# Chunk steps one turn sooner, attention's tile pool split, four kinds of stores on other queues: a change to a hybrid Hyena / mLSTM encoder layer

## The chip, the core and the metric

The kernel runs on one core of a Trainium2 chip. The metric is device time in microseconds (us). The kernel before takes 3098.87 us, the median of 3 runs (3091.53 to 3103.35).

A core has five engines that run side by side, each with its own instruction queue that is worked off in order: TensorE (PE in the profile; PEld are its weight loads), VectorE (DVE), ScalarE (ACT), GpSimd (POOL) and SyncE (SP). In this kernel before the change, SP and ACT are the queues from which transfers are issued; an issue is an instruction like any other, so an engine that waits before an issue holds up everything behind it. SPq and ACTq in the profile are the issuing sides of these two.

## What is computed

One encoder layer, sequence length 2048, model width 1024, all in float32:

```
u = rms_norm(x) ;  P = u @ w_in                      # 1024 x 3600
hy = conv3(P[:, :1536]) ;  spec = filter spectrum(sin-FFN)
y_hy = group_norm( x2 * (h2 * z1 + d2 z1) ),  z1 = x1 * (h1 * v + d1 v)    # long convolutions by FFT
q, k = silu(conv3(P[:, 1536:2560])) ;  v, o, gates = the rest of P
y_ml = group_norm( sigmoid(o) * (mlstm(q,k,v,gates) + mlstm backwards) )  # 4 heads of 128, in chunks
h = x + concat(y_hy, y_ml) @ w_out
h = h + cross_attention(rms_norm(h), rms_norm(mem))  # 4 heads of 256, 256 memory rows
h = h + relu(rms_norm(h) @ ff_w1)^2 @ ff_w2          # 1024 -> 4096 -> 1024
out = rms_norm(h)
```

## The kernel before

Nearly every large product is made from three matmuls: each operand is split into a rounded high half (by ScalarE) and the remainder (by VectorE), and high x high, high x low and low x high are added in PSUM (`mm3`, lines 355 to 361; `split`, line 367).

The kernel is written with Tile: the program allocates tiles from named pools, and a scheduler orders the instructions of every engine from a simulated timeline and puts in the waits. A tile with `bufs=n` has n places that are used in turn. Pools lie on a stack: a pool opened after others were closed takes over their addresses, and its tiles wait until what lay there has been released. A change of a pool or of one step therefore lets the scheduler order all instructions anew.

The program (lines 2078 to 2115) weaves generators. Each `yield` is a turn; `weave(a, b, wa, wb)` takes turns of a and b so that their yielded amounts advance in the ratio wa : wb. The stages that matter here:

- **Input projection** (`sweep`, `natural`): 14 column groups of w_in against the 2048 rows, 1024 rows at a time. `natural` stores the values `vd`, the sigmoid output gate `od` and the gates; its stores of `vd` and `od` go out from ScalarE's queue (line 888). Beside it run the filters, then the Hyena convolution (`hyena`), whose last step stores the normed rows `yh` from SP's queue (line 1058), eight pairs of stores. Every pair touches rows all over the sequence, so the whole of `yh` is complete only with the last.
- **Memory projection** (`memproj`, lines 689 to 742): 8 steps, one for each head's keys and each head's values. A step takes a raw 1024 x 256 weight (`project`, 32 matmuls at line 704), copies the result (`kt`, line 706), multiplies it by a second weight (`keys`, line 721, or `values`, line 733), copies each PSUM bank into a staging tile `o` (tag `st`, 3 places, line 711) and stores it from ScalarE's queue: `gd` for the keys (line 723, 16 stores), `vw` for the values (line 735, 16 stores). The weights (`wm`) come in through SP's queue (line 417), into four places.
- **mLSTM chunks** (`mlstm`, from line 1217): 16 chunks of 128 rows in a chain. One chunk goes through SP loads (lines 1248, 1249, 1168, 1174), matmuls (1274, 1312, 1314, 1190), GpSimd (1280, 1281, 1333), ScalarE (1283, 1317, 1326, 1184) and VectorE (1265, 1284, 1320, 1328, 1196); every second chunk is followed by the norm of two chunks and their stores `ym` (line 1348). The first call of the generator sets the constants up, loads two chunks and makes the first scores; each later call does one chunk.
- **The join**: `take(n, 2)` runs two turns of the memory projection, then `beside_each(n, take(m, 5))` alternates one turn of it with one of the first five of the mLSTM. So four chunks are done when the first block of the next stage wants their 512 rows.
- **Attention** (`attention`, from line 1418), in four blocks of 512 rows. A block turns the rows of `yh` and `ym` by transposes (`mixed`, `rows`, `turn`, lines 1452 to 1477), multiplies by w_out (8 products), then scores, softmax, weighing with `vw`, 8 more products, residual, and `store`, which scales one 128 x 512 piece (`hg`, 2 places, line 1602) and stores it from ScalarE's queue (line 1603, 32 stores in all). Weights come as pairs of 8 KB tiles a partition, `wh` and `wl`, two places each; each 256 KB piece is loaded by SP into a staging tile (`wn`, four places, shared with the rows; the first pair through the tag `e`) and split. The first block starts with the half of its products that needs only `yh` (line 1512).
- The mLSTM's other chunks are woven into the attention by `weave(g, m, 440, 112, True)`.
- **Feed-forward** (`ffn`): 2 x 7 products of a Strassen-like scheme up and down; it fills the last 1200 us.

The pools on the left side of the stack before: `i_sb` holds everything of the input projection and the memory projection (the parameters, `P`, `cv`, `xn`, `wh`, `wl`, `wn`, `st`, ...). Above it lie the small gate columns and `h_sb`, the Hyena's pool. When all these are closed, `t` takes the addresses over, with acc, the second pair of row tiles (`act1`), both weight pairs, and, as they are first used, the first pair of row tiles (`act0`) and `wn`. `t_a` (staging `e`, `hg`, sums) is on top.

Of the kernel before, what the change touches and what calls it, by code (L numbers as in the profile page):

```python
# [20 lines left out]
D = 1024  # L21
# [112 lines left out]
class Prog:  # L134
# [247 lines left out]
    def weights(self, pool, w, n, kc=4, bufs=2, nbufs=2, pin=False):  # L382
# [4 lines left out]
        if n > 512:  # L387
            for k0 in range(kt):
                for c0 in range(0, n, 512):
                    cs = slice(c0, c0 + 512)  # L390
                    nat = pool.tile([128, 512], F32, tag="wn", name="wn", bufs=nbufs)
# [3 lines left out]
        for k0 in range(0, kt, kc):  # L395
            nat = pool.tile([128, kc, n], F32, tag="wn", name="wn", bufs=nbufs)
# [31 lines left out]
    def inproj_open(self, es):  # L428
# [7 lines left out]
        self.d_gt = self.dram("gt", (L, 16))  # L436
        sb = self.isb = es.enter_context(tc.tile_pool(name="i_sb", bufs=1))
# [27 lines left out]
    def square_sum(self, x, dst):  # L465
        junk = self.isb.tile([128, 512], F32, tag="st", name="junk", bufs=3)
        return self.tc.keep_in_program_order(self.nc.scalar.activation(junk, x, AF.Square, accum_out=dst))
# [56 lines left out]
    def x_chunks(self, hf):  # L524
# [3 lines left out]
        def room(n):  # L528
            if not 1 < n < deep:
                return None  # L530
            t = self.isb.tile([128, 1088], F32, tag=("P", "cv")[n % 2], name="xt", bufs=2)
# [16 lines left out]
    def x_first(self):  # L548
# [18 lines left out]
        for j in range(4):  # L567
            t = sb.tile([128, 1088], F32, tag=("P", "cv")[j // 2], name="xt", bufs=2)
# [13 lines left out]
        def squares(xs, c):  # L582
            for k in range(8):
                sq = sb.tile([128, 512], F32, tag="st", name="sq", bufs=3) if k else ssum[c]
# [33 lines left out]
        def second():  # L618
            for k in range(0, 8, 2):
                nat = sb.tile([128, 2, 256], F32, tag="wn", name="wn", bufs=4)  # L620
# [40 lines left out]
    def prep_mem(self):  # L661
# [11 lines left out]
        def halves():  # L673
            xs = [load(h) for h in range(2)]
            by_half = self.dram("rows", (2, 128, 128)).rearrange("i (d s n h) t -> s (i d) n (h t)", d=2, s=2, n=8)
            t = sb.tile([128, 1088], F32, tag="cv", name="rp", bufs=2)[:, 0:D]
# [12 lines left out]
    def memproj(self):  # L689
# [19 lines left out]
        def staged(p):  # L709
            o = sb.tile([128, 2, 256], F32, tag="st", name="o", bufs=3)  # L710
            nc.scalar.copy(o, p)
            return o

        def keys(h, t):
            q = next(self.mst)
            for i2 in range(4):
# [6 lines left out]
                nc.scalar.dma_start(out=gd[h // 2, :, 2 * i2:2 * i2 + 2, cs], in_=staged(p))  # L723
# [20 lines left out]
    def sweep(self, cols, hf, first, after=None):  # L744
# [3 lines left out]
        for run in [cols[:2]] + [[c2] for c2 in cols[2:]] if self.made == 0 else [[c2] for c2 in cols]:  # L748
# [7 lines left out]
            for c, c2 in [(c, c2) for c in range(2) for c2 in run]:  # L756
                wh, wl = ws[c2]
                for m in range(2):
# [11 lines left out]
                    def leave(c=c, m=m, c2=c2, p=p, cc=cc, Ps=Ps, run=run):  # L770
# [19 lines left out]
                        cv = sb.tile([128, 1088], F32, tag="cv", name="cv", bufs=2)  # L790
# [20 lines left out]
    def sweep_out(self, ct, cv, t0, n):  # L811
# [3 lines left out]
        if ct < 12:  # L815
            w = min(n // 8, 128)
            dst = self.d_hy[ct // 4, t0:t0 + 8 * w, cc].rearrange("(q j) c -> q j c", j=8)
            for j4 in range(2):
# [3 lines left out]
                st = sb.tile([128, 4, 128], F32, tag="st", name="st", bufs=3)  # L822
                self.copy(st[0:w], pt[0:w])
                nc.sync.dma_start(out=dst[:, 4 * j4:4 * j4 + 4], in_=st[0:w])
            if n > 8 * w:
                pt = self.mm()
                nc.tensor.transpose(pt[0:16, 0:128], v[:, 8 * w:n], self.ident)
                st = sb.tile([128, 4, 128], F32, tag="st", name="st", bufs=3)
# [7 lines left out]
        for b in range(0, n, 512):  # L836
            pt = self.mm().rearrange("p (k t) -> p k t", k=4)
            st = sb.tile([128, 4, 128], F32, tag="st", name="st", bufs=3)
# [9 lines left out]
            if rest:  # L848
# [3 lines left out]
                st = sb.tile([128, 4, 128], F32, tag="st", name="st", bufs=3)  # L852
# [3 lines left out]
    def natural(self, hf, tiles, after=None, at=4):  # L856
# [3 lines left out]
        for c2 in tiles:  # L860
# [3 lines left out]
            for t in range(8):  # L864
# [18 lines left out]
                so = sb.tile([128, 512], F32, tag="st", name="st", bufs=3)[:, 0:256]  # L883
# [4 lines left out]
                nc.scalar.dma_start(out=(self.d_vd if c2 < 2 else self.d_od)[r0:r0 + 128, 256 * (c2 % 2):256 * (c2 % 2) + 256],  # L888
# [1282 lines left out]
```

## Time and profile before

| | us |
|---|---|
| median of 3 runs | 3098.87 |
| lowest, highest | 3091.53, 3103.35 |
| the profiled execution | 3097.53 |
| its span, first to last instruction | 3095.8 |
| TensorE matmuls busy | 3023.0 |
| VectorE, ScalarE, GpSimd busy | 1952.6, 1500.4, 1130.9 |

The profile page gives one execution. "Busy" is the union of an engine's instructions. The windows view cuts the span into stretches and gives for each engine its busy time (with the number of instructions), the TensorE clock that was granted (1.00 is full speed), the mean busy share of the 16 DMA engines and the GB/s they moved; a share can come out slightly over 1. The view of waits says which engine stood idle before a line and what ended the idle time, with the total, the number of times and the longest, all in us. The chain of waits walks back from the last instruction through what released each step. In a timeline a row has the start, the time taken, the engine, the line, the operation, its tiles, and in brackets the idle time before it and its releaser. The releaser is the semaphore event that came last, so it can be a transfer that has nothing to do with the data.

### The profile page before, as it was taken

What the parts mean: (1) busy time and instruction counts of PE and PEld (TensorE: products, weight loads), DVE (VectorE), ACT (ScalarE), POOL (GpSimd) and SP (SyncE); (2) the same over time, 40 slices, a digit from 0 to 9 for tenths busy, and PEclk for the clock granted to TensorE, in tenths of its full rate; (3) what the DMA queues carried; (4) which work ended last, traced back from release to release, by engine and by line L of the source; (5) the groups of instructions that cost most, each with busy time, mean ns of one, the idle gap of its engine ahead of it and who ended that gap; (6) DMA issues with size and microseconds to landing.
All of it is one profiled execution on the core that took longest, in us unless ns stands there. A gap on an engine that the chain in (4) does not pass through costs nothing.

```text
span 3095.8 us, 42982 instructions
## 1 busy us (share of the span) xinstructions
PE 3023.0 (98%) x14287; PEld 2375.2 (77%) x14287; DVE 1952.6 (63%) x3442; ACT 1500.4 (48%) x2930; POOL 1130.9 (37%) x798
## 2 busy tenths in 40 slices
PE   9999999999999998999999999999999999999998
PEld 7655767776676766888887888888888888888876
DVE  8855465446656456877664666557555686566695
ACT  6443465534656225565544455556555543333335
POOL 0122011200222343333132237766466374244653
PEclk9999999999999999999999999999999999999999
DMA  6554767575867997464476556657544565353434
GB/s 225 187 191 164 243 214 237 178 234 193 260 199 241 301 309 231 151 204 160 149 246 222 183 188 224 210 180 240 196 153 151 183 212 171 109 166 117 159 102 164
DMA packets 444102, 607.07 MB, mean 196 GB/s; under 512 B 38494, under 2 KB 248542, under 8 KB 442856
## 3 DMA queue, kind: packets, MB, share of 16 engines
q1 hardware_dynamic: 405988, 546.54, 55.1%
q10 hardware_dynamic: 37892, 57.79, 5.5%
q8 instruction: 113, 1.85, 0.2%
q14 instruction: 109, 0.89, 0.1%
HBM read 401.79 MB, written 202.41 MB: 195 GB/s over the span
## 4 chain that ended last, share of the span: by engine, by line
PE 82%; DMA 7%; DVE 5%; ACT 2%; issue 2%; POOL 1%; SPq 0%; ACTq 0%; DVEq 0%; POOLq 0%
PE mm L357 17%; PE mm L361 17%; PE mm L360 17%; PE hy L357 6%; PE hy L361 6%; PE hy L360 6%; PE hy L178 3%; PE mm L948 2%; PE hy L979 1%; PE hy L1021 1%; DMA a<-hy 1%; DMA xt<-in_x_t_dram 1%; PE hy L1312 1%; PE mm L733 1%; PE hy L1314 1%
## 5 line engine op out<-in xcount | busy, mean ns | idle before, releaser
L1669 ACT CAST ah<-w 128x512 fp32r<-128x512 f32 x284 | 177.1, 624 | 302.0 <-PE hy L360 155.3
L1670 DVE TENSOR_TENSOR bl<-wr,bh 128x512 fp32r<-128x512 f32 x213 | 238.2, 1123 | 124.7 <-ACT bh L1669 124.7
L368 DVE TENSOR_TENSOR wl<-wn,wh 128x512 fp32r<-128x512 f32 (+1 forms) x296 | 215.4, 773 | 101.1 <-ACT wh L368 100.8
L1026 POOL TENSOR_TENSOR b<-b,a 128x512 f32<-128x512 f32 x64 | 86.8, 1359 | 510.5 <-ACT b L1024 240.8
L357 PE MATMUL mm<-xh,wh 128*128 128x512 f32 x640 | 265.5, 416 | 2.5 <-ACT st L206 1.3
L360 PE MATMUL mm<-xl,wh 128*128 128x512 f32 x640 | 252.9, 395 | 1.8 <-DVE xl L368 1.8
L361 PE MATMUL mm<-xh,wl 128*128 128x512 f32 x640 | 253.6, 397 | 0.0
L1670 DVE TENSOR_TENSOR al<-w,ah 128x512 fp32r<-128x512 f32 x236 | 216.4, 917 | 57.1 <-ACT ah L1669 56.9
L1669 ACT CAST bh<-wr 128x512 fp32r<-128x512 f32 x232 | 143.8, 622 | 223.6 <-PE mm L361 173.8
L361 PE MATMUL mm<-bh,al 128*128 128x512 f32 x576 | 223.7, 391 | 3.8 <-DVE al L1670 3.8
L357 PE MATMUL mm<-bh,ah 128*128 128x512 f32 x576 | 225.8, 392 | 0.8 <-DVE acc L1832 0.7
L360 PE MATMUL mm<-bl,ah 128*128 128x512 f32 x576 | 224.9, 390 | 0.0
L368 ACT CAST wh<-wn 128x512 fp32r<-128x512 f32 (+1 forms) x296 | 165.0, 619 | 104.6 <-PE mm L361 52.6
L360 PE MATMUL mm<-act,wh 128*128 128x512 f32 x512 | 201.8, 394 | 0.0
L361 PE MATMUL mm<-act,wl 128*128 128x512 f32 x512 | 199.3, 391 | 0.4 <-DVE wl L368 0.4
L357 PE MATMUL mm<-act,wh 128*128 128x512 f32 x512 | 198.7, 394 | 1.0 <-ACT wh L368 0.9
L357 PE MATMUL hy<-bh,ah 128*128 128x512 f32 x448 | 175.2, 391 | 0.0
L360 PE MATMUL hy<-bl,ah 128*128 128x512 f32 x448 | 174.6, 390 | 0.0
L361 PE MATMUL hy<-bh,al 128*128 128x512 f32 x448 | 174.4, 390 | 0.0
L357 PEld LDWEIGHTS mm<-xh,wh 128*128 128x128 f32 x640 | 120.1, 188 | 56.0 <-issue 19.2
L357 PE MATMUL mm<-wh,xh 128*128 128x256 f32 (+1 forms) x512 | 155.6, 304 | 3.5 <-ACT xh L368 2.0
L361 PEld LDWEIGHTS mm<-xh,wl 128*128 128x128 f32 x640 | 120.1, 188 | 46.2 <-issue 21.8
(380 smaller groups left out, 8219.6 us busy)
## 6 DMA issues: line engine op xcount, KB each, us to landing
wr<-hc SPq DMA_DIRECT2D x224, 256.0 KB
w<-in_ff_w_dram SPq DMA_DIRECT2D x172, 256.0 KB
hc<-wn SPq DMA_DIRECT2D x128, 256.0 KB
wn<-in_w_in_dram SPq DMA_DIRECT2D x100, 256.0 KB
hc<-q SPq DMA_DIRECT2D x96, 256.0 KB
fs<-a SPq DMA_DIRECT2D x32, 512.0 KB
a<-fs SPq DMA_DIRECT2D x64, 256.0 KB
a<-zs SPq DMA_DIRECT2D x64, 256.0 KB
```

Of the source, the lines that this page charges most:

```text
L178: b = self.nc.tensor.matmul(*products[-1], start=True, stop=True)
L357: first = mm(ps, lh, rh, start=start, stop=False)
L360: mm(ps, lh, rl, start=False, stop=False)
L361: self.last = mm(ps, ll, rh, start=False, stop=stop)
L368: both = (self.nc.scalar.copy(hi, src), self.nc.vector.tensor_tensor(lo, src, hi.bitcast(F32), ALU.subtract))
L733: mul(p, t[:, m, ms], o_[:, m, ds], start=m == 0, stop=m == 1)
L948: nc.tensor.matmul(pp, dm[:, m], t[:, m], start=True, stop=True)
L979: nc.tensor.matmul(pg, em[:, m], y, start=True, stop=True)
L1021: nc.tensor.matmul(pp, dm[:, m], t[:, m], start=True, stop=True)
L1026: nc.gpsimd.tensor_tensor(xt, xt, hi[:, m], ALU.mult)
L1669: self.nc.scalar.copy(hi, src)
L1670: eng.tensor_tensor(lo, src, hi.bitcast(F32), ALU.subtract)
```

## The change

Six edits. The diff is cut to its core; every other use of the tags `st`, `wn` and `cv` in the input projection goes to the new pools in the same way.

1. The input projection's pool is split: `i_w` (tags `cv`, `wn`) at the bottom, then `i_st` (tag `st`), then `i_sb` with the rest.
2. Attention's pool `t` becomes four: `t_w` (the first weight pair) at the bottom, `t_acc`, `t` (the second pair of row tiles and the second weight pair), and `t_n` (the first pair of row tiles, `wn`) on top. Weight pairs alternate between `t_w` and `t`.
3. The stores of `gd`, of `hg` and half of those of `od` (column group 2) move from ScalarE's queue to SP's; those of `yh` move from SP's to GpSimd's. Half of the staged keys use the tag `wn` instead of `st`, so that there are seven places.
4. `take(n, 1)` in place of `take(n, 2)`: each of the first five mLSTM turns comes one turn of the memory projection sooner.
5. `weave(g, m, 440, 140, True)` in place of 112: more mLSTM turns to a product of the attention.
6. In the first block, the first transpose of the `ym` rows is kept in program order.

```diff
+        sw = self.isw = es.enter_context(tc.tile_pool(name="i_w", bufs=1))
+        for tag, n, bufs in (("cv", 1088, 2), ("wn", 544, 4)):
+            for _ in range(bufs):
+                sw.tile([128, n], F32, tag=tag, name=tag, bufs=bufs)
+        self.ist = es.enter_context(tc.tile_pool(name="i_st", bufs=1))
         sb = self.isb = es.enter_context(tc.tile_pool(name="i_sb", bufs=1))
...
-        def staged(p):
-            o = sb.tile([128, 2, 256], F32, tag="st", name="o", bufs=3)
+        def staged(p, wide=False):
+            if wide:
+                o = self.isw.tile([128, 2, 256], F32, tag="wn", name="o", bufs=4)
+            else:
+                o = self.ist.tile([128, 2, 256], F32, tag="st", name="o", bufs=3)
             nc.scalar.copy(o, p)
             return o
...
-                nc.scalar.dma_start(out=gd[h // 2, :, 2 * i2:2 * i2 + 2, cs], in_=staged(p))
+                nc.sync.dma_start(out=gd[h // 2, :, 2 * i2:2 * i2 + 2, cs], in_=staged(p, i2 % 2 == 0))
...
-                nc.scalar.dma_start(out=(self.d_vd if c2 < 2 else self.d_od)[r0:r0 + 128, 256 * (c2 % 2):256 * (c2 % 2) + 256],
-                                  in_=so)
+                (nc.sync if c2 == 2 else nc.scalar).dma_start(
+                    out=(self.d_vd if c2 < 2 else self.d_od)[r0:r0 + 128, 256 * (c2 % 2):256 * (c2 % 2) + 256], in_=so)
...
-                    nc.sync.dma_start(out=yh[g, :, js], in_=sq[own[g]])
+                    nc.gpsimd.dma_start(out=yh[g, :, js], in_=sq[own[g]])
...
     def tail_open(self, es):
-        T = self.T = es.enter_context(self.tc.tile_pool(name="t", bufs=1))
-        self.acc = T.tile([128, 8, 512], F32, name="acc")
+        def pool(name):
+            return es.enter_context(self.tc.tile_pool(name=name, bufs=1))
+
+        self.wp = [pool("t_w"), None]
+        for tag in ("wh", "wl"):
+            self.wp[0].tile([128, 8, 256], F32R, tag=tag, name=tag)
+        self.acc = pool("t_acc").tile([128, 8, 512], F32, name="acc")
+        self.wp[1] = self.ap = pool("t")
         self.acts = 2
         for _ in range(2):
             self.act_tile("act")
         for tag in ("wh", "wl"):
-            for _ in range(2):
-                T.tile([128, 8, 256], F32R, tag=tag, name=tag, bufs=2)
-        self.acts = 0
+            self.wp[1].tile([128, 8, 256], F32R, tag=tag, name=tag)
+        self.T = pool("t_n")
+        self.acts = self.wps = 0
...
+    def pair(self, names):
+        pool = self.wp[self.wps % 2]
+        self.wps += 1
+        return [pool.tile([128, 8, 256], F32R, tag=t, name=n) for t, n in zip(("wh", "wl"), names)]
...
-        def turn(yn):
+        def turn(yn, pin=False):
             pt = self.hy()
             for k in range(4):
-                nc.tensor.transpose(pt[:, 128 * k:128 * k + 128], yn[:, 128 * k:128 * k + 128], self.ident)
+                d = nc.tensor.transpose(pt[:, 128 * k:128 * k + 128], yn[:, 128 * k:128 * k + 128], self.ident)
+                if pin and k == 0:
+                    tc.keep_in_program_order(d)
...
-                self.split(y[0][s2], y[1][s2], turn(yn))
+                self.split(y[0][s2], y[1][s2], turn(yn, c == 0 and n == 4))
...
-                nc.scalar.dma_start(out=hgd[c, :, ct], in_=hg)
+                nc.sync.dma_start(out=hgd[c, :, ct], in_=hg)
...
-                             p.turned_in(), take(n, 2), beside_each(n, take(m, 5)))
+                             p.turned_in(), take(n, 1), beside_each(n, take(m, 5)))
...
-                weave(g, m, 440, 112, True)
+                weave(g, m, 440, 140, True)
```

More of the change, by code (lines that the diff above doesn't have):

```diff
@@ L1693, in ffn_x @@
         if i in (7, 3):
[L1694 to L1695 removed]
+            hi, lo = (t.rearrange("p (k n) c -> p k (n c)", n=2) for t in self.pair(("xh", "xl")))
         else:
```

38 lines of the change are left out of this document (17 added, 21 removed).

## The prediction

> **What bounds the kernel now.** First the page's head, then the windows, cut at the edges of the stages.
>
> ```profile
> span 3095.8 us, 42982 instructions
> PE 3023.0 (98%) x14287; PEld 2375.2 (77%) x14287; DVE 1952.6 (63%) x3442; ACT 1500.4 (48%) x2930; POOL 1130.9 (37%) x798
> ...
> core 0: us, PE busy (x) PEld busy (x) DVE busy (x) ACT busy (x) POOL busy (x), PEclk, DMA share, GB/s
> 0.00:950.00 950.00, 931.25 (x4533) 655.23 (x4534) 581.65 (x1078) 492.18 (x843) 141.58 (x103) 1.00 0.67 211
> ...
> 1050.00:1130.00 80.00, 70.72 (x310) 51.59 (x309) 36.69 (x106) 17.71 (x45) 28.66 (x21) 0.96 1.05 365
> 1130.00:1178.80 48.80, 48.80 (x220) 32.95 (x218) 26.46 (x90) 21.91 (x72) 18.28 (x15) 1.00 0.73 237
> 1178.80:1205.00 26.20, 13.99 (x84) 13.06 (x84) 20.61 (x59) 16.50 (x57) 10.79 (x8) 0.74 0.83 276
> 1205.00:1318.00 113.00, 112.85 (x618) 97.39 (x617) 89.31 (x240) 61.11 (x189) 39.60 (x29) 1.00 0.51 158
> 1318.00:1332.00 14.00, 9.25 (x53) 7.75 (x52) 11.65 (x33) 12.29 (x43) 3.78 (x3) 0.88 0.63 189
> 1332.00:1860.00 528.00, 525.80 (x2579) 439.20 (x2578) 345.61 (x703) 270.89 (x631) 163.59 (x116) 1.00 0.59 194
> ```
>
> TensorE is busy for 98% of the span, so all idle time together is 3095.8 − 3023.0 = 72.8 us, and the change takes no matmul away. What it can win lies where it acts: the memory projection (1050 to 1130), with 9.3 us idle; the join to the attention (1178.8 to 1205), with 12.2; the end of the first block (1318 to 1332), with 4.75. In these three the granted clock is also low, at 0.96, 0.74 and 0.88. Counting a clock of c as a loss of 1 − c of the busy time, that is 2.8, 3.6 and 1.1 us more. At stake are 12.1, 15.8 and 5.9 us, 33.8 in all. The stretches between have no idle time to give: 0.15 us in 1205 to 1318, 2.2 in 1332 to 1860.
>
> The low clock is seen in single rows: the same 16 matmuls take 3.72 us before a gap and 5.37 behind it.
>
> ```profile
> 1054.34 3.72 PE L721 MATMUL mm<-kt,wm 128*128 128x256 f32 x16 [0.79 <-ACT o L711]
> ...
> 1060.89 5.37 PE L721 MATMUL mm<-kt,wm 128*128 128x256 f32 x16 [2.83 <-ACT kt L706]
> ```
>
> Next, who TensorE waited for from 1030 to 1340 (total, times, longest).
>
> ```profile
> PE hy L1190 <- ACT ht L1326: 7.6, 1, 7.6
> PE hy L1460 <- DMA wn<-yh: 4.4, 1, 4.4
> PE hy L1460 <- DVE act L368: 3.1, 2, 2.8
> PE mm L721 <- ACT kt L706: 2.8, 1, 2.8
> PE mm L721 <- ACT o L711: 2.2, 2, 1.4
> PE mm L704 <- ACT o L711: 1.9, 1, 1.9
> ```
>
> The last three belong to the memory projection and name ScalarE, which is busy there for only 17.71 of 80 us. Its timeline says why it is late.
>
> ```profile
> 1055.37 0.57 ACT L711 COPY o<-mm 128x512 f32<-128x512 f32 x1
> 1059.64 0.37 ACTq L723 DMA_DIRECT2D gd<-o  x1
> 1060.06 0.31 ACT L213 ACTIVATE brm<-ms,eps 128x16 f32<-128x16 f32 x1 [4.12 <-DMA a<-hy]
> 1060.27 0.57 ACT L706 COPY kt<-mm 128x512 f32<-128x512 f32 x1
> ...
> 1088.96 0.59 ACT L711 COPY o<-mm 128x512 f32<-128x512 f32 x1
> 1099.73 0.37 ACTq L723 DMA_DIRECT2D gd<-o  x1
> 1100.19 0.59 ACT L711 COPY o<-mm 128x512 f32<-128x512 f32 x1 [10.64 <-DMA wm<-in_xa_wo_dram]
> ```
>
> A copied tile is ready at 1055.94, but its store is issued at 1059.64; behind it the queue holds the next `kt`, and TensorE stands. The releaser, a load of the Hyena's gate, shares no data with `gd`. I read it, as an inference, as a count of finished transfers that a new issue waits on and shares with unrelated ones. At a DMA share of 1.05 those land late, up to 10 us.
>
> At the join the chain of waits shows two holds one after the other.
>
> ```profile
> 1178.08 3.78 DMA vw<-o
> ...
> 1181.94 0.32 SPq L1454
> ...
> 1185.31 6.42 DMA acc<-in_x_t_dram
> ...
> 1193.26 2.10 PE hy L1190 x8
> ```
>
> and around them stand these rows of SP and ScalarE.
>
> ```profile
> 1153.32 2.40 SPq L1058 DMA_DIRECT2D yh<-a  x2
> ...
> 1159.95 1.64 SPq L1385 DMA_DIRECT2D we<-in_w_out_dram  x3
> ...
> 1181.94 1.74 SPq L1454 DMA_DIRECT2D wn<-yh  x4
> 1184.10 2.17 ACT L368 CAST wh<-we 128x512 fp32r<-128x512 f32 x4
> ```
>
> The first weights are issued at 1159.95 but split only at 1184.10, and the `yh` rows, stored from 1153.32 to 1155.72, are fetched at 1181.94: both wait until the memory projection's last store lands. The fourth chunk runs alone in that gap, with nothing for TensorE beside it.
>
> **The change part by part.** Sums are against the profiled execution, 3097.5 us around a span of 3095.8. It lies 1.3 under the median of 3098.87, which I add at the end.
>
> *Stores of `gd` on SP, seven staging places.* ScalarE issues 16 fewer transfers there.
>
> ```profile
> L723 ACTq DMA_DIRECT2D gd<-o x16: 366/366/435, 1053.2 to 1128.3; - x16
> ...
> L888 ACTq DMA_DIRECT2D od<-st x32: 326/327/696, 500.9 to 1023.4; - x32
> ...
> L1603 ACTq DMA_DIRECT2D hg<-hg x32: 326/326/442, 1353.1 to 1839.5; - x32
> ...
> L1058 SPq DMA_DIRECT2D yh<-a x16: 456/467/1762, 1060.2 to 1155.1; - x16
> ```
>
> The issue time is little (16 x 0.366 = 5.9 us, on an engine that idles); what matters is that holds of 4 and 10 us no longer sit ahead of the copies. They move to SP, where the loads of `wm` stand behind them, and seven places instead of three carry the copies over. The three waits on ScalarE come to 2.8 + 2.2 + 1.9 = 6.9 us. Upper bound: all 12.1. There is a floor under the stage, too: from 1050 to 1178.8 the transfers moved 365 x 80 + 237 x 48.8 = 40.8 MB. The sooner chunk and the sooner `yh` rows bring some ten pieces of 256 KB forward, so about 43.3 MB, which at 365 GB/s take 119 us of the 128.8: no more than 10 us can be won here. Lower bound 0, the transfers as the limit. I take 6.9, since exactly these waits hang on ScalarE.
>
> *`yh` on GpSimd.* The trace has no transfer issued there. The nearest rows are those of the same store on SP: 16 x 0.467 = 7.5 us at the median, 16 x 1.762 = 28 at the longest, on an engine that is busy for 28.66 + 18.28 = 47 of 128.8 us. Behind a store wait GpSimd's multiplies for the chunks and the Hyena. On the path lies only the last pair: 1155.72 to 1181.94 are 26 us of cover, against two issues of up to 3.5 us. Cost 0; 3.5 if the cover is used up by rows fetched as soon as they can be. SP loses the same 16 issues, which pays for the 16 of `gd`.
>
> *`od` and `hg` on SP.* ScalarE saves 16 x 0.327 + 32 x 0.326 = 15.7 us, none of it on the path, since TensorE is full where they run. Value 0; the loss it can bring is the third rival.
>
> *The pools and the sooner chunks.* The first weight pair lies where `cv` and `wn` were, which the memory projection leaves early, and rows and first operands lie above `i_sb`. So splitting and transposing can happen before 1178. One turn of the memory projection is some 128.8 / 8 = 16 us, so the fourth chunk, whose last matmuls now end at 1195.4, falls under the last steps; the 12.2 us of idle time are its waits and those for the operands. Late next is the second weight pair, whose place is still freed by the last step: four casts of 2.17 us in all, then the remainders, against 24 matmuls of two half products, which at 525.80 us for 2579 take 4.9. Of the 15.8 us I take 12, and leave 3.8 for that and for a clock that may sag. Bounds: 6, if only the chunk moves and the operands come as late as now, and 15.8.
>
> *More chunk turns in the first block, and the pinned transpose.* Eleven chunks are spread over 66 x 440 / 140 = 207 units of attention instead of 66 x 440 / 112 = 259, a quarter denser. VectorE is already busy 89.31 of 113 us there. If half of that is the chunks', it rises by 11 to 100: near full, with short waits for TensorE. I take a loss of 2 us, bounds 0 and 8. The pin can hold TensorE until the rows land, 4.4 us as in the one wait on such a load. It comes after the first half products, so 0.
>
> *The wait of 4.4 us in 1318 to 1332* is for rows whose staging places are full of weights. The places stay four; 0, bounds −6 and +6.
>
> *A new order everywhere.* In 0 to 950 TensorE idles 18.75 us in small waits that are dealt out anew; I put 0, with 4 either way.
>
> Sum: 6.9 + 12 − 2 = 16.9 us. 3097.5 − 16.9 + 1.3 = **3082 us**; by the bounds above, 3066 to 3100.
>
> **The rivals.** *The transfers are the limit (3089).* At a share of 1.05 a store that leaves ScalarE's queue still needs the same bytes moved, the holds come back as late weights, and only the join gains: 3097.5 − 12 + 2 + 1.3 = 3089. For it speaks the 1.05; against it that no wait of TensorE in the stage names a load of weights. The Trainium skill, "DMA: Bandwidth & Descriptors", section "Issuing engines are not separate DMA queues", says that transfers issued by different engines run on the same DMA engines and that spreading them saves only issuing time. By that rule the stores' move is worth nothing here; the ScalarE rows above disagree in so far as the price was not the issue but the holding of the queue.
>
> *Both stretches gain in full (3073).* 3097.5 − 10 − 15.8 − 0 + 1.3 = 3073; with the 4.4 us wait also gone, 3068. It needs the second weight pair in time and a clock that never drops.
>
> *`hg` behind SP's holds, slower (3120).* SP stands for staging places:
>
> ```profile
> SPq L1385 <- DVE wl L368: 157.5, 105, 10.8
> ...
> ACT hg L1602 <- DMA hg<-hg: 8.8, 6, 2.6
> ```
>
> With two places of `hg`, two products of 4.9 us cover a store that is late; ScalarE was already held 2.6 us by it. Take 2.6 for the landing: a hold beyond 9.8 − 2.6 = 7.2 us makes ScalarE wait before `hg`, the casts of the next weights stand behind it, and TensorE after them. At the longest hold, 10.8, that is 3.6 us for each of the 16 weight pairs in those products, 58 us; if two in three of them meet it, 38. Result 3082 + 38 = 3120. It decides once most loads ahead of an `hg` store wait over 7.2 us. Against it: the mean is 157.5 / 105 = 1.5.
>
> *The change doesn't do what it says (3095).* The split pools still wait for the last landing because the scheduler puts the casts late; the chunk alone moves, the denser turns cost 2: 3097.5 − 6 + 2 + 1.3 = 3095.
>
> **How the numbers follow.** Chances: forecast 0.54, transfers as the limit 0.17, full gain 0.07, `hg` slower 0.13, not as it says 0.09. A measurement of this kernel tells about 0.5% from no change, which is 15.5 us: faster is below 3083.4, slower above 3114.4. Of the forecast's 0.54 some 0.37 lie below 3083.4, and of the first rival 0.04; with the full gain and 0.02 from spill of the rest that is 0.50. Slower: `hg`, and 0.02 for anything that ties GpSimd or SP up worse, 0.15. The rest, 0.35, is the same. The forecast's own range is 3066 to 3100; for 8 in 10 I go to 3106 above, which leaves out most of the `hg` case.
>
> **What would show it.** In the windows: 1050 to 1130 with idle time near 3 us and the clock near 1.00, ScalarE's rows without a hold ahead of `kt` (stores right); the join without a gap over 3 us and the cast of `wh<-we` before the last `vw` store (pools right); the fourth chunk's matmuls among those of line 733 (chunks right). Wrong would be TensorE waits for `wm` loads in the memory projection, waits of `hg` on its own store over 10 us in total, GpSimd issues of `yh` above 2 us each, or new idle time over 5 us in 1205 to 1318.

## The result, and the profile after

The changed kernel takes 3110.7 us, the median of 11 runs (3107.06 to 3118.22), against 3099.25 for the kernel before beside it: a ratio of 1.0033, 95% interval 1.0025 to 1.0041. By that ratio it is 10.2 us slower (the two medians alone differ by 11.5), where 16.9 us faster was forecast. Its profiled execution took 3109.76 us around a span of 3107.7.

In what follows line numbers are those of the kernel after: `mm<-kt,wm` of the keys is line 729 there, `kt` 711, the staged copy 719, the store of `gd` 731, the values 741, the rows 1471, their transposes 1477, the stores of `yh` 1066 and of `hg` 1622. First the page's head and the windows at the cuts of the prediction.

```profile
span 3107.7 us, 43038 instructions
...
PE 3026.9 (97%) x14287; PEld 2375.7 (76%) x14287; DVE 1945.5 (63%) x3442; ACT 1498.1 (48%) x2930; POOL 1145.5 (37%) x814
```

```profile
core 0: us, PE busy (x) PEld busy (x) DVE busy (x) ACT busy (x) POOL busy (x), PEclk, DMA share, GB/s
...
1050.00:1130.00 80.00, 75.51 (x340) 55.55 (x339) 35.21 (x104) 17.32 (x48) 30.44 (x27) 0.98 1.04 346
1130.00:1178.80 48.80, 44.43 (x209) 29.34 (x208) 30.98 (x105) 20.91 (x66) 24.37 (x21) 0.97 0.79 271
1178.80:1205.00 26.20, 14.35 (x69) 12.14 (x68) 15.17 (x45) 15.58 (x55) 8.70 (x9) 0.61 0.81 272
1205.00:1318.00 113.00, 110.02 (x611) 94.88 (x610) 88.39 (x248) 63.41 (x206) 46.26 (x32) 0.98 0.50 155
...
1332.00:1860.00 528.00, 515.46 (x2497) 428.98 (x2498) 328.61 (x673) 260.75 (x604) 146.85 (x104) 0.99 0.57 187
```

The reader is to see three things. In 1050 to 1130 the idle time fell from 9.3 to 4.5 us, but in 1130 to 1178.8, which was full, 4.4 us are idle now. The memory projection is done sooner (its last matmuls start at 1167.3 for 1176.5); from its start near 1019 to this end TensorE idles 6.8 us for 9.6, so it did gain, by 2.8 us of idle time. The join, 1178.8 to 1205, is as idle as before (11.9 us for 12.2), at a lower clock (0.61 for 0.74). And 1332 to 1860, where the prediction changes nothing in its sum, went from 2.2 to 12.5 us idle. That is 10.3 of the 11.9 us by which the two spans differ, and the other stretches nearly cancel: it is the next thing to open. The waits of TensorE in 1495 to 1545, the turn to the third block of the attention (total, times, longest):

```profile
PE hy L1477 <- DMA wn<-ym: 3.4, 1, 3.4
PE mm L361 <- DVE wl L368: 2.6, 1, 2.6
PE mm L357 <- ACT e L1578: 2.5, 1, 2.5
```

Before, the same stretch has one wait, of 0.2 us. What stands in front is seen in SP's timeline of the kernel after,

```profile
1490.80 0.47 SPq L1683 DMA_DIRECT2D wr<-hg  x1
...
1496.73 3.84 SPq L1735 DMA_DIRECT2D w<-in_ff_w_dram  x3
...
1509.43 1.99 SPq L1726 DMA_DIRECT2D w1s<-w  x4
1519.05 0.32 SPq L1471 DMA_DIRECT2D wn<-yh  x1
1519.42 0.43 SPq L1735 DMA_DIRECT2D w<-in_ff_w_dram  x1
1519.94 1.40 SPq L1471 DMA_DIRECT2D wn<-yh  x3
```

and of the kernel before, where the two rows below are neighbours:

```profile
1487.21 2.12 SPq L1385 DMA_DIRECT2D wn<-vw  x4
1504.40 2.25 SPq L1454 DMA_DIRECT2D wn<-yh  x4
```

Lines 1683, 1726, 1735 and 1778 belong to the feed-forward: its first operands (`wr`), its first weights (`w`) and their saved sums (`w1s`). They are wanted some 350 us later (the last matmul of the attention's last product starts at 1848.9), but SP issues 24 of these transfers from 1490.80 on, ahead of the rows of the third block, which go out 15 us later than before. The kernel before loads its first feed-forward weights at 1554.3, by the view of that line (shortest, median and longest issue in ns, first and last start):

```profile
L1717 SPq DMA_DIRECT2D w<-in_ff_w_dram x112: 368/384/1685, 1554.3 to 2394.6; - x112
```

ScalarE is caught in the same way (in brackets the idle time and its releaser):

```profile
1494.94 0.62 ACT L1688 CAST bh<-wr 128x512 fp32r<-128x512 f32 x1 [7.51 <-DMA wr<-hg]
...
1511.71 0.56 ACT L1578 ACTIVATE e<-mm,mx,qr_y 128x256 f32<-128x256 f32 x1 [4.29 <-DVE mx L1575]
```

It stands 7.5 us before a cast for the feed-forward, whose operand is not there yet, and the softmax (line 1578) comes behind such work on two engines: its step at 1511.71 waits for VectorE's `mx`, and VectorE has subtractions for the feed-forward (line 1689) in front, at 1506.63 and 1510.23. The Trainium skill, "PSUM — Partial Sum Buffer", section "Engine vs sequencer instructions", says that the queues of ScalarE, VectorE and GpSimd are strictly first in, first out. The rows agree: nothing overtook the waiting cast.

Then the join to the attention. The last rows of `yh` leave GpSimd so (its timeline):

```profile
1171.56 2.50 POOL L1064 TENSOR_TENSOR a<-a,ghy 128x512 f32<-128x512 f32 x2 [7.99 <-DVE a L1062]
...
1178.94 1.12 POOL L1066 DMA_DIRECT2D yh<-a  x2
```

and SP fetches them, and the first weights, so:

```profile
1185.66 1.74 SPq L1471 DMA_DIRECT2D wn<-yh  x4
1187.44 2.15 SPq L1403 DMA_DIRECT2D we<-in_w_out_dram  x4
```

Before, `yh` was complete in issue at 1155.72, 26 us ahead of the fetch. Now its last pair is multiplied 21 us later than before (1171.56 for 1150.61), stands 4.9 us behind four multiplies of a chunk and leaves 24 us later. Two chunk turns, whose scores start at 1140 and 1168, fell between the last two Hyena turns. The first weights, issued behind the rows (1187.44, three of the four were at 1159.95 before), are cast later than before, at 1193.76 for 1184.10, and long after the last store of the memory projection:

```profile
1168.58 0.37 ACTq L743 DMA_DIRECT2D vw<-o  x1
...
1193.76 0.62 ACT L368 CAST wh<-we 128x512 fp32r<-128x512 f32 x1 [4.07 <-DMA we<-in_w_out_dram]
```

The fourth chunk did come sooner (its last matmuls of this stretch start at 1183.12 for 1193.26), but the first product of the attention starts only 4 us sooner, at 1200.3 for 1204.4. TensorE's waits in 1030 to 1340 show it:

```profile
PE hy L1477 <- DMA wn<-yh: 4.7, 2, 3.6
PE hy L1477 <- DVE act L368: 4.6, 1, 4.6
PE hy L178 <- DMA a<-zg: 4.5, 2, 2.8
...
PE mm L741 <- ACT kt L711: 2.1, 1, 2.1
```

Of the memory projection's waits for ScalarE, 6.9 us together, 2.1 are left; a load of the Hyena's gate (`a<-zg`) has come in with 4.5.

### The profile page after: what moved, and what is told of

Same layout as the page of the kernel before. It is cut to its first block, busy times and chain, and to the rows that moved or that the text cites. A ratio compares the mean times of both kernels' runs of the same rounds, so it can differ in the third digit from the quotient of the medians.

```text
span 3107.7 us, 43038 instructions
## 1 busy us (share of the span) xinstructions
PE 3026.9 (97%) x14287; PEld 2375.7 (76%) x14287; DVE 1945.5 (63%) x3442; ACT 1498.1 (48%) x2930; POOL 1145.5 (37%) x814
## 4 chain that ended last, share of the span: by engine, by line
PE 50%; DVE 3%; DMA 2%; issue 1%; ACT 1%; POOL 0%; SPq 0%; DVEq 0%; ACTq 0%; POOLq 0%
PE mm L357 10%; PE mm L361 10%; PE mm L360 10%; PE hy L361 6%; PE hy L360 6%; PE hy L357 6%; DVE bl L1689 0%; DMA hg<-hg 0%; DVE al L1689 0%; DMA wr<-in_ff_w_dram 0%; DVE acc L1987 0%; DMA wr<-xs 0%; PE hy L1320 0%; PE hy L1322 0%; DMA w<-in_ff_w_dram 0%
## 5 line engine op out<-in xcount | busy, mean ns | idle before, releaser
L368 DVE TENSOR_TENSOR wl<-wn,wh 128x512 fp32r<-128x512 f32 (+1 forms) x296 | 206.4, 742 | 103.4 <-ACT wh L368 103.2
```

What stands on the lines that cost most here:

```text
L368: both = (self.nc.scalar.copy(hi, src), self.nc.vector.tensor_tensor(lo, src, hi.bitcast(F32), ALU.subtract))
```

## The experiments

Each kernel ran beside the kernel before on the same chip, five rounds; ratios are to that one, with their 95% interval. The medians of the kernel before were 3098.97 to 3101.18 us in these rounds, so differences between kernels are taken from the ratios and not from the medians; 0.001 is 3.1 us.

**The denser chunks: what do they cost, and by which way?** Theory A, from the rows above: with 140 the last chunk ends some 50 us sooner (the last matmul of a chunk starts at 1472.9 for 1525.7), `ms.close()` gives the mLSTM's pool back, and the scheduler puts the feed-forward's first work into the place that has come free, in front of the third block. Theory C: the denser chunks themselves load VectorE. e1 takes 140 out of the kernel after, e4 puts it alone into the kernel before.

```diff
# e1_w112, against the kernel after
-                weave(g, m, 440, 140, True)
+                weave(g, m, 440, 112, True)
# e4_only140, against the kernel before
-                weave(g, m, 440, 112, True)
+                weave(g, m, 440, 140, True)
```

> The changed kernel with the old weaving ratio (112 in place of 140), all other edits kept. Theory A (the mLSTM ends some 40 us sooner, its pool is free sooner, and the feed-forward's first loads and splits move into the join of the third attention block, where TensorE idles 9.0 us at a clock of 0.94): the idle time of that join falls under 2 us, the third block's rows are fetched before any load of ff_w1, and the time is 10 us less, 3100 us. Theory C (the loss comes from the denser chunks themselves in the first block): only the 3.0 us idle and the clock of 0.97 there go, about 5 us less, 3105 us, and the third join still stalls. Theory B (the prediction's rival: hg behind SP's holds): no more than 2 us change.

> The kernel before with one edit alone, the ratio of 140 for 112. Theory A: the stall of 9 us at the third block's join appears here, too, and the time is 3107 to 3111 us. Theory B and the view that the pools or the stores are at fault: 3099 us, no stall there.

Measured: e1 3097.79 us, 0.9995 (0.9986 to 1.0004); e4 3113.21, 1.0044 (1.0031 to 1.0056). Taken out it gives 11.8 us, put in alone it costs 13.6. Where, the windows of e4 tell: the first block with its denser chunks is full,

```profile
1205.00:1330.00 125.00, 124.86 (x703) 108.62 (x702) 102.78 (x289) 72.97 (x241) 52.53 (x37) 0.99 0.54 167
```

and 9.9 of the 40 us behind 1500 are idle:

```profile
1500.00:1540.00 40.00, 30.12 (x141) 23.68 (x140) 29.71 (x47) 18.19 (x41) 12.85 (x9) 0.96 0.77 252
```

VectorE was indeed busy for 102.78 of 125 us, as the prediction feared, and TensorE did not wait for it. To part A from C by an intervention, e8 keeps the 140 but holds the pool.

```diff
# e8_hold, against the kernel after
                 weave(g, m, 440, 140, True)
+                held = 0
+                while held < 52:
+                    held += next(g)
+                p.nc.gpsimd.tensor_copy(p.gcols[:, 0, 0:8], p.acc[:, :, 0])
                 ms.close()
```

The copy writes a tile of the mLSTM's pool and reads what an addition of the attention wrote, so the pool is released only behind both.

> The kernel after, with 140 as it is, but the mLSTM's right-side pool is given back only after 52 more units of attention have been emitted, about where the weave by 112 ends, and behind a small copy on GpSimd that reads what attention's last addition before that point wrote. The chunks stay as dense as in the kernel after. Theory A (the pool is free sooner, so the feed-forward's first loads, casts and stores are put in front of the third block's rows and softmax): the idle time at 1510 to 1530 goes, and the time comes to 3097 to 3101 us, as with 112. Theory C (the denser chunks themselves load VectorE and ScalarE): nothing changes, 3108 to 3112 us.

Measured: 3097.52 us, 0.9989 (0.9979 to 0.9998), 13.6 us from the kernel after, with chunks as dense (the last matmul of a chunk starts at 1471.8). Its SP now has the rows first and the feed-forward behind them, at 1532, right behind the copy, which runs at 1531.84:

```profile
1507.97 2.78 SPq L1471 DMA_DIRECT2D wn<-yh  x4
...
1532.06 1.27 SPq L1683 DMA_DIRECT2D wr<-hg  x3
```

The same window is full, against 31.04 busy of 40 in the kernel after:

```profile
1500.00:1540.00 40.00, 39.37 (x196) 32.45 (x195) 23.37 (x46) 21.30 (x47) 3.42 (x4) 1.00 0.42 129
```

Theory A is shown: not the density but the early release costs. In 1332 to 1860 e8 idles 3.3 us where the kernel after idles 12.5, so 9.2 of the 13.6 us are seen there; where the rest lies is not shown. Of the times expected, e4's lies 2 us above its range.

**The stores.** e5 and e3 undo one queue each in the kernel after.

```diff
# e5_hg_act, against the kernel after
-                nc.sync.dma_start(out=hgd[c, :, ct], in_=hg)
+                nc.scalar.dma_start(out=hgd[c, :, ct], in_=hg)
# e3_yh_sp, against the kernel after
-                    nc.gpsimd.dma_start(out=yh[g, :, js], in_=sq[own[g]])
+                    nc.sync.dma_start(out=yh[g, :, js], in_=sq[own[g]])
```

> The kernel after with the stores of hg back on ScalarE. Theory B (hg stores behind the sync engine's waits for staging places hold ScalarE): faster by 4 us or more, 3100 to 3107. Rival (the two places of hg cover the delay, as the trace after shows no long wait of ScalarE on hg): 3108 to 3113.

> The changed kernel with the yh stores on SP again. If GpSimd's issues (0.56 us each in the trace, with the multiplies of the next pair behind them) make the Hyena's tail late, the last yh store is issued before 1165 us and the time is 3105 us. If they do not, the tail stays within 5 us of 1178.9 and the time within 3 us of 3110.7.

Measured: e5 3112.13 us, 1.0036 (1.0024 to 1.0048), no different from the kernel after. ScalarE's wait before `hg` is in the kernel after

```profile
ACT hg L1621 <- DMA hg<-hg: 8.8, 5, 4.3
```

with the 8.8 us in total that it had before; the longest is 4.3 for 2.6. SP's holds add nothing to that total, and the third rival of the prediction has fallen. e3: 3107.13, 1.0023 (1.0013 to 1.0033), 3.1 us from the kernel after. Neither of its two expectations came out whole: the last store of `yh` starts at 1176.0 for 1179.5, so the tail stays late without GpSimd's issues, and the time lies outside both. The issues of `yh` on GpSimd (minimum, median and longest in ns, then the landing in us),

```profile
L1066 POOL DMA_DIRECT2D yh<-a x16: 537/562/739, 1049.2 to 1179.5; - x16
...
DMA to landing us min/median/max: 4.8/6.6/8.1
```

are cheap, a quarter of the 2 us that would have counted as wrong. The 4.9 us that the last pair stands behind a chunk's multiplies are more, but e3 takes back only 3.5 us of the last store's start. e9 asks whether the two costs add up, by undoing both.

```diff
# e9_112_sp, against the kernel after
-                weave(g, m, 440, 140, True)
+                weave(g, m, 440, 112, True)
-                    nc.gpsimd.dma_start(out=yh[g, :, js], in_=sq[own[g]])
+                    nc.sync.dma_start(out=yh[g, :, js], in_=sq[own[g]])
```

> The kernel after with 112 and the stores of yh back on the sync engine. If the two costs found so far are independent, 3097.8 - 3.6 = 3094 us (3092 to 3096). If the issuing on GpSimd only costs while the first block is dense: 3097 to 3099.

Measured: 3093.5 us, 0.9981 (0.9972 to 0.9990). Against e1 GpSimd's issue costs 4.3 us here. In both pairs the intervals overlap, so 3 to 4 us is a hint and not more, and by which way it would cost is not shown: in e9 the last store of `yh` starts no sooner than in e1 (1177.9 for 1177.5), and the first product of the attention starts later (1201.4 for 1199.0). From e9, which is the change without its two losses, one more store is put back; the seven staging places stay.

```diff
# e12_gd_act, against e9_112_sp
-                nc.sync.dma_start(out=gd[h // 2, :, 2 * i2:2 * i2 + 2, cs], in_=staged(p, i2 % 2 == 0))
+                nc.scalar.dma_start(out=gd[h // 2, :, 2 * i2:2 * i2 + 2, cs], in_=staged(p, i2 % 2 == 0))
```

> The kernel after with 112, yh on the sync engine (3093.5 us as such) and the stores of gd back on ScalarE, their seven staging places kept. If the memory projection's gain reaches the end of the kernel: 7 to 10 us slower than 3093.5, 3100 to 3104. Theory E (what the memory projection gains is waited away in the join, which ends when the last rows of yh have landed, 24 us later than before the change): 3092 to 3097.

Measured: 3103.19 us, 0.9999 (0.9990 to 1.0009), 5.6 us slower than e9 (7 to 10 were expected): the gain of the memory projection does reach the end. Its last matmuls start at 1179.9 for 1172.6 in e9, and the first product of the attention at 1207.9 for 1201.4. In 1030 to 1168 TensorE waits for ScalarE again in the memory projection,

```profile
PE mm L729 <- ACT kt L711: 3.4, 2, 2.6
...
PE mm L709 <- ACT o L719: 2.0, 1, 2.0
PE mm L729 <- ACT o L719: 1.8, 4, 0.7
```

7.2 us, against 2.1 in e9:

```profile
PE mm L741 <- ACT kt L711: 1.2, 1, 1.2
PE mm L709 <- ACT o L719: 0.9, 1, 0.9
```

The longest of them, 2.6 us, stands behind a held store: a copy is ready at 1062.33, its store is issued 3.5 us later, and the next `kt` comes behind that.

```profile
1061.75 0.58 ACT L719 COPY o<-mm 128x512 f32<-128x512 f32 x1 [4.46 <-DMA wm<-in_xa_wk_dram]
1065.78 0.37 ACTq L731 DMA_DIRECT2D gd<-o  x1
...
1066.40 0.57 ACT L711 COPY kt<-mm 128x512 f32<-128x512 f32 x1
```

By the rule of the Trainium skill that the prediction weighed ("DMA: Bandwidth & Descriptors", "Issuing engines are not separate DMA queues") the move saves issuing time only; the trace disagrees as before, since what came free is TensorE's wait behind a held queue. That the 5.6 us lie near the 5.9 of issuing time says nothing for the rule, since ScalarE is busy for only 24.6 us of 1030 to 1130 in e12.

**The join.** e7 takes the pools alone; e2 and e13 put the chunks back to their old step.

```diff
# e7_pools: the kernel before with the new pools and the pinned transpose
# (112, take(n, 2), every store on its old queue, three staging places)
# e2_take2, against the kernel after; e13_9_take2, the same against e9_112_sp
-                             p.turned_in(), take(n, 1), beside_each(n, take(m, 5)))
+                             p.turned_in(), take(n, 2), beside_each(n, take(m, 5)))
```

> The kernel before with only the split pools, the pinned transpose and the new places of weights and operands: 112, the fourth chunk's step as before, and every store on the queue it had. Prediction's step (operands can be ready before the last store, so the join gains): 3088 to 3092 us. Theory D (in the run with two chunk turns the splits of the first weights stand on VectorE and ScalarE ahead of the fourth chunk, and VectorE waits 8.4 us on a cast whose weights have not landed, so sooner operands hold up the chunk that sets the end): slower than before by 5 to 12 us, 3105 to 3112. If neither the one nor the other binds: 3097 to 3102.

> The changed kernel with take(n, 2) again, so that the chunks come as before. Theory A1 (the sooner chunks take turns from the Hyena's tail, its last pair of yh is stored 24 us later, and the first weights and rows wait for that): the last yh store is issued near 1155 us instead of 1178.9, the join loses less than 8 us instead of 14.1, and the time is 3103 to 3106 us. Rival (the tail is late for another reason, the stores of yh on GpSimd or of gd on SP): the tail stays late, the chunks come late too, and the time is 3113 us or more.

> The kernel after with 112, yh on the sync engine (3093.5 us as such) and the chunks of the memory projection at their old step, behind the second turn. If the sooner chunk is worth here what it was worth in the kernel after (3120.15 against 3110.7): 3101 to 3105. If its worth hung on the dense first block: 3092 to 3096.

Measured: e7 3097.24 us, 0.9996 (0.9987 to 1.0005); e2 3120.15, 1.0070 (1.0056 to 1.0083); e13 3107.19, 1.0021 (1.0012 to 1.0031), 2 us above its range; e2 fits neither of its two expectations whole, the time that of the rival, the tail that of A1. The pools by themselves are worth nothing, and theory D, that they harm, falls with them. Yet e7 does bring what the prediction asked for: the cast of the first weights starts 17 us sooner than before, ahead of the last `vw` store, and TensorE stands in the join all the same (10.0 us idle in 1178.8 to 1205), above all before a transpose, for VectorE's split of the rows.

```profile
1166.60 0.62 ACT L368 CAST wh<-we 128x512 fp32r<-128x512 f32 x1 [1.38 <-DMA we<-in_w_out_dram]
...
1179.95 0.37 ACTq L743 DMA_DIRECT2D vw<-o  x1
```

```profile
PE hy L1477 <- DVE act L368: 6.9, 1, 6.9
```

A1, that the old step would be better, falls too: in e2 the last store of `yh` starts at 1163.2, 16 us sooner than in the kernel after, as A1 has it, and the kernel is slower for all that. The sooner step is worth 11.5 us in the kernel after and 12.4 in e9. But e9 is only 5.9 us faster than before in all, so pools and stores without the sooner step lose 6.5 (e13). What the stores of `gd` are worth thus hangs on the order around them: 5.6 us won beside the sooner step, while without it pools and stores together lose. What sooner operands do there is seen in e2: SP issues four row loads and four weight loads at 1168 to 1177, with the chunk's `va` among them. TensorE's longest wait in 1160 to 1220 is

```profile
PE hy L1320 <- DVE hy L221: 10.9, 1, 10.9
```

and that one stands on two others, of VectorE and of ScalarE:

```profile
DVE wl L368 <- ACT wh L368: 8.4, 1, 8.4
ACT ve L1192 <- DMA va<-vd: 8.0, 2, 5.7
```

VectorE has taken up the split of the first weights and waits for a cast, which ScalarE has behind a chunk's load; the norm that the next chunk needs comes after. Here a sooner operand has been turned into a wait of a chunk in the join.

Theory E was then that the join ends with the last `yh`. It would fall to a Hyena that runs a little ahead:

```diff
# e11_tail304 and e11_tail309 (309), f2_tail300 (300), against e9_112_sp
# f1_before304, against the kernel before; f3_304_take2: e13_9_take2 with 304
-                weave(rest, p.hyena(hs), 499, 297, True)
+                weave(rest, p.hyena(hs), 499, 304, True)
```

> The kernel after with 112 and yh on the sync engine (3093.5 us as such), with the Hyena run 2.4% ahead in its weave with the projections (304 for 297), so that its last rows of yh are stored some 20 us sooner than at 1177.4. Theory E (the join ends with the last yh): the wait for the rows of yh, 7.5 us, goes, and the time is 3086 to 3090 us. Rival (the join's transfers and the chunk that runs in it set its end, at a DMA share of 1.00): 3091 to 3097.

> The same with 309 for 297, the Hyena 4% ahead. Theory E: 3084 to 3090 us. Rival: 3091 to 3097; if the Hyena comes to stand ahead of its own filters or gates, slower than that.

> The kernel before with the Hyena 2.4% ahead (304 for 297) and nothing else changed. Theory E (the lead pays back what the sooner chunk took: the late tail of yh, which before the change is stored at 1155 and waits for nothing): the kernel before gains nothing, 3096 to 3104 us. Rival (the lead is a gain of its own, or a new order that happened to come out well): 3086 to 3092.

> The kernel after with 112, yh on the sync engine and the Hyena 1% ahead (300 for 297). Theory E, the join's end follows the last yh store until that is no longer last: between 297 (0.9981 of before) and 304 (0.9956), so 0.996 to 0.998. If each new order is dealt anew: anywhere from 0.994 to 1.001.

> The kernel after with 112, yh on the sync engine, the Hyena 2.4% ahead and the chunks of the memory projection at their old step. If the sooner chunk was worth 12 us only because it fills the join (two chunks stand alone there without it, and the tail of yh is no bound in either): 1.000 to 1.003 of before. If the lead does the same work as the sooner chunk: 0.995 to 0.998.

Measured, with three starts from each trace (us: the last store of `yh`, the last matmul of the memory projection, the first product of the attention):

| kernel | median us | ratio to before | last yh | last of mem. proj. | first product |
|---|---|---|---|---|---|
| before | 3099.25 | 1 | 1155.1 | 1176.5 | 1204.4 |
| e7 pools alone | 3097.24 | 0.9996 (0.9987 to 1.0005) | 1153.6 | 1174.3 | 1202.1 |
| e9 | 3093.5 | 0.9981 (0.9972 to 0.9990) | 1177.9 | 1172.6 | 1201.4 |
| e13, old step | 3107.19 | 1.0021 (1.0012 to 1.0031) | 1167.6 | 1172.1 | 1217.5 |
| f2, 300 | 3103.41 | 1.0014 (1.0005 to 1.0023) | 1159.1 | 1172.9 | 1212.6 |
| e11, 304 | 3088.04 | 0.9956 (0.9943 to 0.9969) | 1149.4 | 1155.8 | 1197.7 |
| e11, 309 | 3095.31 | 0.9979 (0.9970 to 0.9988) | 1154.5 | 1163.5 | 1202.4 |
| f1, before with 304 | 3086.67 | 0.9960 (0.9947 to 0.9972) | 1132.2 | 1151.5 | 1195.7 |
| f3, 304 and old step | 3084.54 | 0.9957 (0.9945 to 0.9970) | 1135.1 | 1152.8 | 1196.4 |

In e9 TensorE's longest wait in 1165 to 1260 is for the rows of `yh`:

```profile
PE hy L1477 <- DMA wn<-yh: 7.5, 1, 7.5
```

With 304 and with 309 it is gone, as theory E has it, and the first time is right, 3088. The second is wrong. With 300 the last `yh` leaves 19 us sooner than in e9, and the kernel is 10 us slower. And f1, which should have stayed at 3096 to 3104, gains 12.3 us by the lead alone. Theory E has fallen: the lead pays nothing back. It is a gain of its own, or only an order that happens to come out well; the runs do not part these two. On top of it neither pools, nor stores, nor the sooner step are worth anything that can be told (0.9960, 0.9957, 0.9956). In e11_tail304 the waits of TensorE (1030 to 1240) are

```profile
PE hy L1320 <- DVE rw L1292: 7.4, 1, 7.4
PE hy L1477 <- DVE act L368: 5.0, 1, 5.0
PE hy L1320 <- DVE ht L1354: 4.4, 1, 4.4
```

so the idle time of the join has only changed its name: the rows are there, and the chunks (the first and the last line) and the transposes wait for VectorE. f1 has the same pair, `hy` 8.2 and `act` 4.9:

```profile
PE hy L1312 <- DVE bry L218: 8.2, 1, 8.2
PE hy L1460 <- DVE act L368: 4.9, 1, 4.9
```

From 297 over 300 and 304 to 309 the ratio goes 0.9981, 1.0014, 0.9956, 0.9979. That is no curve of a lead; each value lets the scheduler deal the chunks, the Hyena and the loads anew, and 300 even leaves the range of 0.994 to 1.001 that was expected for that. The 4 us to each side that the prediction allowed for a new order are too little: from one value to the next it is 7 to 18 us. Why 304 is good and 300 bad is left open, and that 304 was among the values tried is luck. It also bounds what the single edits above can show: a difference of 3 to 12 us in the time alone may be the new order's, so the edits stand where the traces show the waits that went (the release of the pool, the stores of `gd`), and not by their times.

## Why the prediction was wrong

From forecast to result it is 27 us: 16.9 faster became 10.2 slower.

*The denser chunks, "a loss of 2 us, bounds 0 and 8": measured 11.8 to 13.6.* This is the step that failed first. It looked for the price in the first block, in VectorE, and VectorE took the load: e4 idles 0.14 us in 1205 to 1330, and the one wait of 2.4 us for VectorE that the kernel after has there is in e1, with 112, too. The change of 112 to 140 also moves `ms.close()` and with it the start of everything that takes the pool over, some 200 us behind the stretch where its price was looked for. What the runs showed in place of the 2 us is the stall of the third block behind early feed-forward work. That the feed-forward's first load came at 1551.4, some 26 us behind the last matmul of a chunk at 1525.7, could have been read off the trace of before. None of the marks at the end of the prediction lay there, and so none of its "wrong" marks came true: no waits for `wm`, 8.8 us before `hg`, 0.739 us at most for an issue of GpSimd, 3.0 us idle in 1205 to 1318. The marks for being right did fail: 4.5 us idle in 1050 to 1130 for some 3, gaps of 3.6 and 4.6 us in the join, the cast of the first weights behind the last `vw` store, and the fourth chunk's matmuls (1175.87 to 1183.12 and later) behind the projection's last at 1167.3.

*The stores of `gd`, 6.9 us: right in mechanism, 5.6 in e12, beside the sooner step.* The idle time up to the projection's end fell by 2.8 us only; a wait of 4.5 for the Hyena's gate came in. The first rival, the transfers as the limit, did not come true in the form that it named: no wait for `wm`, at a share of 1.04 for 1.05 and 346 GB/s for 365, and the waits for ScalarE went all the same. But the gate is a late transfer too, so that rival is not wholly out. The reading that the queue was held by transfers of others is borne out as far as the move pays; the count that is shared stays an inference.

*The join, 12 of 15.8 us: failed.* Pools and sooner chunks with `hg` and `od`, but without the stores of `gd` and `yh` and without the 140, are e12, at 0.9999: worth 0, below the lower bound of 6. The step reckoned that idle time in the join is the waits it could name. In e7 the operands are early, and the time stays; the chunk turns and the split of the rows stand there with their own chain, and operands that are early can stand before them in the queues of VectorE and ScalarE (e2). In the kernel after the operands are not even early, since the rows of `yh` and the loads come later. The sooner chunk alone, without the pools, was not tried. What the change gains here and in the memory projection together is e9's 5.9 us, for 18.9 in the sum.

*`yh` on GpSimd, 0, or 3.5 "if the cover is used up": 3 to 4, a hint.* The cover was used up, by a route that the text did not see: the last pair is 24 us late, and the sooner chunk, one turn of the same change, makes 16 of them in the kernel after (e2) and 10 in e9 (e13). But the pair is as late with the stores on SP (e3, e9), so the agreement with 3.5 is luck as far as the runs show. Two edits were priced each against the order of the other's absence.

*`hg` and `od` on SP, 0:* right for `hg` (e5); `od` and the pinned transpose were not tried by themselves.

*The wait of 4.4 us for rows, 0:* it went with the 140 (the kernel after, e4 and e8 don't have it, e1 has), and a wait of 3.2 for VectorE came in its place.

The range of 3066 to 3100 takes fewer of the bounds than the text names. With the lossy end of each (0 for `gd`, 6 for the join, 8 for the chunks, 3.5 for `yh`, 6 for the rows, 4 for a new order) the sum is 3097.5 + 1.3 − 6 + 8 + 3.5 + 6 + 4 = 3114, and 3110.7 lies below that.

The parts as measured: e9 −5.9, GpSimd +4.3, the 140 +11.8, together +10.2. They are steps of one path from the kernel before to the kernel after and must add up to the result; each would measure otherwise in another order of steps (the 140 costs 13.6 when put in first).

## What to carry to other kernels

An edit that finishes a generator sooner also frees its pool sooner, and a scheduler that fills free places will put far-off prefetch in front of near work; look at what opens behind the `close()`, not only at the stage that grows denser. Where the early finish is wanted, delay the release by a real dependency (e8: one small copy won 13.6 us back). Before crediting a join with its idle time, ask what TensorE would have to do in it once the named waits are gone. And try the cheap control: one number in a weave gave the kernel before 12.3 us with nothing else, more than the six edits without their losses. Which number does it only a run tells: of 300, 304 and 309 one lost.

## What the runs showed of the hardware

A store of 256 KB issued by GpSimd held that engine for 0.54 to 0.74 us, 0.56 at the median, not much more than SP's 0.47 for the same store (whose longest is 1.76), and landed 4.8 to 8.1 us after its issue, at DMA shares of 0.79 to 1.04. The Trainium skill, "DMA: Bandwidth & Descriptors", section "Anatomy of one DMA — SWDGE (gpsimd) path", fits the time of such a transfer by 2.0 us and the bytes over 436e3, which for 262144 bytes gives an estimate of 2.6 us; in these loaded stretches the measured time is two to three times as long.

The granted clock was low where TensorE idled: 0.61 in the join with 11.9 of 26.2 us idle, 0.96 in e4 behind 1500 with 9.9 of 40, and 1.00 in e8's same window with 0.6. The idle time alone does not fix it: before the change the join had 0.74 with 12.2 us idle. Counted as the prediction does, e4's stall of 9.9 us costs about one more, by estimate 30.12 x 0.04 = 1.2 us.
